# A gated short-convolution layer on one core: the first tile's shift and scale taken alone, the order of SyncE and VectorE in the first twelve passes written out, and half-size first pieces

## The chip, the cores and the metric

One Trainium2 core runs the whole layer in float32 inputs and outputs. The metric is the device time of one execution in microseconds (us), lower is better; of several runs the median is given. The engines are named as in the profile: PE (TensorE), DVE (VectorE), ACT (ScalarE), POOL (GpSimd), SP (SyncE, which issues almost all DMAs).

## The reference, cut to what matters

The depth is one, so only the short-convolution mixer runs, on 256 tokens of width 2048, with 4096 inner columns:

```
h = rmsnorm(x, norm_g)
shift, scale, gate = split(silu(c) @ ada_w + ada_b, 3)
h = h * (1 + scale) + shift
b, cg, v, g = split(h @ w_in, 4)          # w_in: 2048 x 16384
y = b * causal_conv3(cg * v) * silu(g)
x = x + gate * (y @ w_out)                # w_out: 4096 x 2048
out = rmsnorm(x, final_g)
```

The weights w_in (128 MB), ada_w (48 MB) and w_out (32 MB) are each read once.

## The kernel before, in words

**Products.** Every float32 product is made of three: a tile of weights is split into a rounded part `hi` (ACT, `split_hi`, L356) and a rest `lo` (DVE, `split_lo`, L361), the tokens likewise into `hh` and `hl` (both in the tile that the profile calls hT), and PE adds hi by hh, hi by hl and lo by hh in PSUM (`product`, L496). One such product has 128 x 128 weights and 256 tokens. The width of 2048 makes 16 token tiles, k = 0 to 15.

**Shift and scale of a token tile** are two rows of `silu(c) @ ada_w`, summed over the 16 row blocks of ada_w. For tiles 0 and 1 this is the front of the kernel: their 18 transfers are loaded first (L233), DVE multiplies and adds the row blocks up in `gv0` (L413, L415), PE sums four of the blocks (1, 11, 13 and half of 15) and at last `gv0` itself over the partitions into `sums0` (`sum0`, L394), DVE adds the bias into `mod` (`add_biases`, L326). Then ACT makes hh of both tiles from the normalised tokens `xs` (`high_tokens`, L330); DVE finishes tile 0 (`low_tokens`: xs at L334, hl at L337), and ACT (L429) and POOL (L433) finish tile 1. All of this is held in the order of the program by `in_order` (its last instruction on each engine is kept in `ended`).

The tiles from 2 on come in seven groups of two. `ada_piece` loads a piece of two row blocks by two transfers of 256 KB (L464), DVE adds them up (two operations a piece, L476 and L478), and after eight pieces `ada_done` has PE sum the group over the partitions (four transposes `tp_g`, L486), DVE reduce it (L487) and add the bias (L326), and `modulate` makes hh (ACT, L330) and hl (DVE, L334, L337).

**Passes.** While tiles become ready, PE works on one half of the columns (4 chunks by 4 quarters, 16 sums) in passes. A pass (`part`) loads weights for the tiles that are ready (`raw_s`, L540), splits them, makes the products in a PSUM bank `mm_s` and keeps the sum in SBUF (`keep`: ACT copies at L518, or DVE adds at L520; a pass may instead be seeded from the kept sum at L530). The first thirteen passes take tiles 0 and 1 alone: 24 products from 512 KB of weights each. The next three take four tiles, 48 products from one transfer of 1 MB each. After these 16 the same sums are taken up again for later tiles. Passes are counted here from 1; pass 1 uses weights loaded in the front (`raw0`, L198). Two passes of 512 KB share one buffer of 1 MB (`places`), of which there are three; of the `at` buffers of the ada pieces there are four.

**What sets the order.** `plan()` writes out once the order of pieces and passes. The scheduler, which orders each engine's instructions by priority and by its own timing, may leave that order: the DVE sums of a piece carry a lower priority (`later(GIVE)`), `ada_done` a higher one, and `behind` holds the splits of a pass behind one named instruction: hi behind the kept sum of three passes before, lo of the fourth and fifth pass behind a piece's sums (`added`). Between SP's loads of weights and of ada pieces there is no rule but that. After the passes PE makes the other half of the columns (`mm_b`, 3072 products), then the product with w_out (L738).

Of the kernel before, what the change touches and what calls it, by code (L numbers as in the profile page):

```python
# [8 lines left out]
F32 = mybir.dt.float32  # L9
# [4 lines left out]
P = 128  # L14
# [103 lines left out]
def short_conv_layer(ctx: ExitStack, tc: tile.TileContext, x, c, norm_g, ada_w, ada_b, w_in, conv_w, w_out, final_g, out):  # L118
# [44 lines left out]
    after = mybir.DependencyInfo(mybir.DependencyClass.NoSync, mybir.DependencyReason.DATA)  # L163

    @contextmanager
    def in_order():

        traced = nc.cur_bb.bb.instructions
        n = len(traced)
        yield  # L170
        last = {}
        for ins in list(traced[n:]):
            if ins.engine in last:
                tc.add_manual_dep(ins, last[ins.engine], after, reason="in order")
            last[ins.engine] = ins.name
        ended.update(last)

    @contextmanager
    def behind(last):
# [209 lines left out]
    def sum0(k, rows, col, halves=(0, 1)):  # L389


        for o in range(2 * NK0):
            if o // NK0 in halves:
                nc.tensor.matmul(  # L394
                    sums0[:, o * P : (o + 1) * P], rows[:, o // NK0, (o % NK0) * P : (o % NK0 + 1) * P],
                    col.to_broadcast([P, P]),
                    start=k == ON_PE[0] and o == 0, stop=k is None, skip_group_check=True,
                )

    for k in range(KT):  # L400
        c_k = silu_c[:, k : k + 1]
        at, gv = first_ada[k], gv0
        if k in ON_PE:
            if k == 11:
                for j in range(3):
                    keep_x(j, turn_x(j))
                tp_3 = turn_x(3)
            sum0(k, at, c_k, (0,) if k == KT - 1 else (0, 1))
            if k < KT - 1:
                continue  # L410
            at, gv = at[:, 1], gv0[:, 1]
        if k == 0:
            nc.vector.tensor_scalar_mul(gv, at, c_k)  # L413
        else:
            nc.vector.scalar_tensor_tensor(out=gv, in0=at, scalar=c_k, in1=gv, op0=ALU.mult, op1=ALU.add)  # L415
    for half in range(2):
        sum0(None, gv0, ones[:, 0:1], (half,))
    blocks0 = [raw0[:, k * CT * P : (k + 1) * CT * P] for k in range(NK0)]
    hi0 = [split_hi(b, CT * P) for b in blocks0]
    add_biases(0, NK0, sums0.rearrange("p (o f) -> p o f", o=2 * NK0)[:, :, 0])  # L420
    pieces0 = []
    for k in range(NK0):
        high_tokens(k)
    for k in range(NK0):
        if k == 0:
            pieces0.append(split_lo(blocks0[k], CT * P, hi0[k]))
            low_tokens(k)
        else:
            nc.scalar.activation(  # L429
                xs[0][:, k, :], xs[0][:, k, :], AF.Identity, bias=mod[:, 0, k : k + 1], scale=mod[:, 1, k : k + 1]  # L430
            )
            pieces0.append(split_lo(blocks0[k], CT * P, hi0[k]))
            nc.gpsimd.tensor_tensor(out=hl_[k], in0=xs[0][:, k, :], in1=hh_[k].bitcast(F32), op=ALU.subtract)  # L433
    pinned.close()

    def conv(ct, u, cv):
# [34 lines left out]
    def ada_sums(j, kk, at4, gv):  # L471
        for i in range(kk):
            c_k = silu_c[:, j + i : j + i + 1]
            if j + i == 0:
                with behind(ended):
                    nc.vector.tensor_scalar_mul(gv, at4[:, i], c_k)  # L476
            else:
                nc.vector.scalar_tensor_tensor(out=gv, in0=at4[:, i], scalar=c_k, in1=gv, op0=ALU.mult, op1=ALU.add)  # L478
        added.append({ins.engine: ins.name for ins in nc.cur_bb.bb.instructions[-1:]})

    def ada_done(k0, nk, gv):

        tp = psum.tile([P, 4, P], F32, tag="sm", name="tp_g", bufs=2)
        gs = const.tile([P, 4], F32, tag="gs", name="gs", bufs=2)
        for o in range(2 * nk):
            nc.tensor.transpose(tp[:, o, :], gv[:, o // nk, (o % nk) * P : (o % nk + 1) * P], ident)  # L486
        nc.vector.reduce_sum(gs[:, 0 : 2 * nk], tp[:, 0 : 2 * nk, :], axis=mybir.AxisListType.X)  # L487
        modulate(k0, nk, gs[:, 0 : 2 * nk])

    opener = [None]  # L490

# [20 lines left out]
    kept, added = [], []  # L512

    def keep(ch, q, k0, bank, seed=False):
        if k0 == 0 or seed:
# [6 lines left out]
    def part(ch, q, k0, k1, seed):  # L522


        col = q * E + ch * CT * P
        step = SLOT // (CT * P)
        first = k0
        bank = psum.tile([P, CT, T], F32, tag="mm", name="mm_s")
        if seed:
            nc.scalar.copy(bank, acc[ch, q])  # L530
        if pieces0:
            for k in range(NK0):
                chunk_products(bank, *pieces0[k], 0, k, k0, k1, late=True)
            pieces0.clear()
            k0 = NK0
        for s0 in range(k0, k1, step):
            sk = min(step, k1 - s0)
            n = sk * CT * P
            raw, hi, lo = places(n)
            nc.sync.dma_start(  # L540
                raw[:, :n].rearrange("p (k f) -> p k f", k=sk),
                w_in[0, s0 * P : (s0 + sk) * P, col : col + CT * P].rearrange("(k p) f -> p k f", p=P),
            )
            at = len(acc) if k0 == 0 else KT
            with behind(ended if at < 3 else kept[at - 3] if at < 9 else {}):
                split_hi(raw, n, hi)
            with behind(ended if at < 3 else added[at - 3] if at < 5 else {}):
                split_lo(raw, n, hi, lo=lo)
            for parts in ((0, 1), (2,)) if 0 < len(acc) < 3 else ((0, 1, 2),):
                for i in range(sk):  # L550
                    chunk_products(bank, hi, lo, i * CT * P, s0 + i, k0, k1, seed, parts=parts)
        if len(acc) == 1:
            with behind(ended):
                keep_x(3, tp_3)
        keep(ch, q, first, bank, seed)
        kept.append({ins.engine: ins.name for ins in nc.cur_bb.bb.instructions[-1:]})
# [14 lines left out]
            split_y(ys[-1], vq)  # L571

    LATER = (10, 14)
    whole = [0] * NCH
    for kind, *step in plan():
        if kind == "ada":
            ada_piece(*step)
        else:
            ch, k1 = step[0], step[3]
            part(*step)  # L580
            if step[2] == 0 and len(acc) in LATER:
                with tc.issue_after(last_mm[0].ins), behind(ended):
                    if len(acc) == LATER[0]:
                        rows2 = rows_tile("rows2")
                        nc.gpsimd.dma_start(rows2[:, :], conv_w.rearrange("w (k p) -> (w k) p", p=P))
                    else:
                        turn(rows2, 0, 96, cw)
            whole[ch] += k1 == KT
            if k1 == KT and whole[ch] == 4:
                mixed(ch)  # L590
# [354 lines left out]
```

## Time and profile before

| | |
|---|---|
| three runs | 902.77, 903.24 (median), 905.11 us |
| profiled execution | 903.37 us |
| its span, first to last instruction | 901.6 us |
| mean granted TensorE clock | 0.997 |
| PE busy | 887.4 us, 98% |
| first product of a pass | 25.01 us after the span's start |
| passes on the first half of the columns | to 378.57 us |
| the second half, mm_b | 348.16 us, 3072 products |

The profile is of one execution. A row of a timeline gives start, duration, engine, source line, operation, output and inputs, and in brackets the idle time before it and what ended that. Times are from the span's start; outside the span the profiled execution has another 1.8 us. PE is busy nearly all the time, so what can be gained or lost is time at which PE waits.

### The profile page before, as it was taken

The numbers are of one execution on the slowest core, as the hardware profiler recorded it, in microseconds if no ns is written. First come the engines' busy times: TensorE is split into PE (matmuls) and PEld (weight loads), VectorE is DVE, ScalarE is ACT, GpSimd is POOL, SyncE is SP. The second block draws the span as 40 slices with busy tenths as digits, with TensorE's granted clock in tenths as the row PEclk, the third lists the DMA queues.
The fourth block names the chain that finished last, engine by engine and source line by source line (L and its number), as shares of the span: only waits on it lengthen the run. The fifth ranks groups of instructions, "written<-read, shape, count | busy, mean of one in ns | idle before, by whom it ended". The sixth has DMA issues, their size and how long they took to land.

```text
span 901.6 us, 16416 instructions
## 1 busy us (share of the span) xinstructions
PE 887.4 (98%) x6997; PEld 850.6 (94%) x6997; DVE 675.3 (75%) x665; ACT 484.9 (54%) x429; POOL 84.8 (9%) x96
## 2 busy tenths in 40 slices
PE   7999999999999999999999999999999999999996
PEld 4899999999999999999999999999999988888885
DVE  5889989888888867765775678565555568879886
ACT  6768866665548856644443434444434445554543
POOL 0000000000000042024224302420000000000000
PEclk9999999999999999999999999999999999999998
DMA  9999999999998588687978898866666476673662
GB/s 307 365 369 368 368 315 348 356 369 352 351 326 289 165 277 250 192 257 229 295 227 247 256 289 269 240 198 197 201 193 188 141 284 222 199 275 123 203 234 94
DMA packets 159610, 235.01 MB, mean 261 GB/s; under 512 B 6900, under 2 KB 105284, under 8 KB 159152
## 3 DMA queue, kind: packets, MB, share of 16 engines
q1 hardware_dynamic: 156368, 226.52, 76.7%
q0 software_dynamic: 3040, 7.39, 2.8%
q8 instruction: 55, 0.90, 0.4%
q14 instruction: 19, 0.16, 0.1%
q10 hardware_dynamic: 128, 0.04, 0.0%
HBM read 224.49 MB, written 2.10 MB: 251 GB/s over the span
## 4 chain that ended last, share of the span: by engine, by line
PE 95%; DMA 3%; SPq 0%; ACT 0%; DVE 0%; issue 0%; ACTq 0%; DVEq 0%
PE mm_b L496 39%; PE mm_s L496 37%; PE mm_w L738 7%; PE mm_o L738 7%; PE mm L738 4%; DMA at<-in_ada_w_dram 2%; DMA x<-in_x_dram 1%; PE tp_g L486 0%; DVE lo L361 0%; SPq L464 0%; ACT hi L356 0%; ACT acc L518 0%; SPq L540 0%; SPq L218 0%; ACT big L852 0%
## 5 line engine op out<-in xcount | busy, mean ns | idle before, releaser
L496 PE MATMUL mm_s<-hT,hi 128*128 128x256 f32 x2048 | 348.4, 277 | 1.1 <-ACT hT L330 1.1
L496 PE MATMUL mm_b<-hT,hi 128*128 128x256 f32 x2048 | 348.2, 276 | 0.0
L496 PEld LDWEIGHTS mm_s<-hT,hi 128*128 128x128 f32 x2048 | 307.2, 188 | 1.3 <-ACT hT L330 1.3
L496 PEld LDWEIGHTS mm_b<-hT,hi 128*128 128x128 f32 x2048 | 308.2, 188 | 0.0
L496 PE MATMUL mm_b<-hT,lo 128*128 128x256 f32 x1024 | 282.8, 276 | 0.0
L496 PE MATMUL mm_s<-hT,lo 128*128 128x256 f32 x1024 | 280.2, 277 | 0.8 <-DVE lo L361 0.8
L356 ACT CAST hi<-raw 128x2048 fp32r<-128x2048 f32 (+1 forms) x66 | 123.7, 1875 | 193.5 <-PE mm_b L496 156.7
L361 DVE TENSOR_TENSOR lo<-raw,hi 128x2048 fp32r<-128x2048 f32 (+1 forms) x66 | 150.4, 2280 | 99.9 <-ACT hi L356 99.3
L496 PEld LDWEIGHTS mm_b<-hT,lo 128*128 128x128 f32 x1024 | 192.2, 188 | 0.0
L496 PEld LDWEIGHTS mm_s<-hT,lo 128*128 128x128 f32 x1024 | 190.7, 188 | 1.2 <-DVE lo L361 1.2
L361 DVE TENSOR_TENSOR lo<-raw_s,hi 128x2048 fp32r<-128x2048 f32 (+1 forms) x80 | 149.5, 1877 | 35.1 <-ACT hi L356 34.6
L356 ACT CAST hi<-raw_s 128x2048 fp32r<-128x2048 f32 (+1 forms) x80 | 124.2, 1558 | 58.2 <-PE mm_s L496 47.2
L478 DVE SCALAR_TENSOR_TENSOR gv<-at,silu_c,gv 128x512 f32<-128x512 f32 x105 | 78.5, 748 | 7.6 <-DMA at<-in_ada_w_dram 5.9
L518 ACT COPY acc<-mm_s 128x1024 f32<-128x1024 f32 x54 | 54.7, 1013 | 39.4 <-PE mm_s L496 39.2
L361 DVE TENSOR_TENSOR lo<-raw_o,hi 128x2048 fp32r<-128x2048 f32 x22 | 50.4, 2290 | 23.4 <-ACT hi L356 23.4
L356 ACT CAST hi<-raw_o 128x2048 fp32r<-128x2048 f32 x22 | 42.0, 1908 | 46.4 <-PE mm_w L738 12.6
L738 PE MATMUL mm_w<-hi,y 128*128 128x512 f32 x184 | 58.8, 389 | 0.0
L634 POOL TENSOR_TENSOR gacc<-gacc,z 128x512 f32<-128x512 f32 x28 | 44.7, 1597 | 116.2 <-DMA z<-gacc 116.2
L738 PE MATMUL mm_o<-hi,y 128*128 128x512 f32 x176 | 55.3, 389 | 0.0
L628 DVE SCALAR_TENSOR_TENSOR gacc<-at_g,silu_c,gacc 128x512 f32<-128x512 f32 x60 | 45.8, 764 | 8.2 <-DMA at_g<-in_ada_w_dram 7.2
L632 POOL DMA_DIRECT2D z<-gacc x28 | 15.6, 556 | 330.5 <-DVE acc L569 283.9
L738 PEld LDWEIGHTS mm_w<-hi,y 128*128 128x128 f32 x184 | 34.5, 188 | 7.2
(154 smaller groups left out, 689.4 us busy)
## 6 DMA issues: line engine op xcount, KB each, us to landing
raw<-in_sc_w_in_dram SPq DMA_DIRECT2D x64, 1024.0 KB, 5.8
raw_s<-in_sc_w_in_dram SPq DMA_DIRECT2D x47, 1024.0 KB, 8.3
raw_o<-in_sc_w_out_dram SPq DMA_DIRECT2D x32, 1024.0 KB, 5.3
at<-in_ada_w_dram SPq DMA_DIRECT2D x126, 256.0 KB, 7.9
raw_s<-in_sc_w_in_dram SPq DMA_DIRECT2D x33, 512.0 KB, 7.2
at_g<-in_ada_w_dram SPq DMA_DIRECT2D x32, 512.0 KB, 8.1
x<-in_x_dram SPq DMA_DIRECT2D x4, 512.0 KB, 6.3
big<-in_x_dram SPq DMA_DIRECT2D x2, 1024.0 KB, 8.2
```

Of the source, the lines that this page charges most:

```text
L356: nc.scalar.copy(hi[:, :n], raw[:, :n])
L361: last_low[0] = nc.vector.tensor_tensor(out=lo[:, :n], in0=raw[:, :n], in1=hi[:, :n].bitcast(F32), op=ALU.subtract)
L478: nc.vector.scalar_tensor_tensor(out=gv, in0=at4[:, i], scalar=c_k, in1=gv, op0=ALU.mult, op1=ALU.add)
L496: mm = last_mm[0] = nc.tensor.matmul(dst, w, h[k], start=begins and left, stop=ends, skip_group_check=True)
L518: nc.scalar.copy(acc[ch, q], bank)
L628: nc.vector.scalar_tensor_tensor(out=ga, in0=at3[:, i, :], scalar=s, in1=ga, op0=ALU.mult, op1=ALU.add)
L632: nc.gpsimd.dma_start(turned[0 : P - away], ga[away:P])
L634: nc.gpsimd.tensor_tensor(out=ga, in0=ga, in1=turned, op=ALU.add)
L738: nc.tensor.matmul(dst, y[a], b, start=opens and i == 0, stop=ends and i == 2, skip_group_check=True)
```

## The change

It has three parts.

1. **Front.** Tile 0 is taken alone. PE adds the last row block for tile 0 in shift and scale, and DVE for tile 1; `first_bias(0)` sums tile 0's part of gv0 over the partitions and adds its bias, then DVE itself makes hh of tile 0 from the tokens. ACT makes xs of tile 0 afterwards. Tile 1 follows: POOL makes its tokens (a tensor_scalar in place of the subtraction at L433), ACT rounds them into hh, and the lo parts and hl of both tiles are DVE's.
2. **Order.** From the second step of the plan to the twelfth pass SP and DVE follow the program's order, so the two sums of an ada piece stand on DVE, and its loads on SP, where the plan has them. The holds of the fourth and fifth pass behind `added` go; the lo parts of pass 15 are held behind the first later group's last token operation (`turned_to`).
3. **Pieces.** In the first 16 passes a piece is at most 512 KB, so passes 14 to 16 load and split twice 512 KB in place of once 1 MB.

```diff
-    def in_order():
+    def in_order(engines=None):
...
+            if engines is not None and ins.engine not in engines:
+                continue
...
-        ended.update(last)
+        if engines is None:
+            ended.update(last)
...
-            sum0(k, at, c_k, (0,) if k == KT - 1 else (0, 1))
+            sum0(k, at, c_k, (0,) if k == KT - 1 else range(NK0))
...
-            at, gv = at[:, 1], gv0[:, 1]
+            at, gv = at[:, :, P : NK0 * P], gv0[:, :, P : NK0 * P]
...
+    def first_tokens(k, engine, out):
+        engine.tensor_scalar(
+            out=out, in0=xs[0][:, k, :], scalar1=mod[:, 1, k : k + 1], scalar2=mod[:, 0, k : k + 1],
+            op0=ALU.mult, op1=ALU.add,
+        )
+    def first_rest(k):
+        pieces0.append(split_lo(blocks0[k], CT * P, hi0[k]))
+        nc.vector.tensor_tensor(out=hl_[k], in0=xs[0][:, k, :], in1=hh_[k].bitcast(F32), op=ALU.subtract)
...
+    first_bias(0)
+    hi0.append(split_hi(blocks0[0], CT * P))
+    first_tokens(0, nc.vector, hh_[0])
+    nc.scalar.activation(xs[0][:, 0, :], xs[0][:, 0, :], AF.Identity, bias=mod[:, 0, 0:1], scale=mod[:, 1, 0:1])
+    for k in range(1, NK0):
+        first_bias(k)
+        first_tokens(k, nc.gpsimd, xs[0][:, k, :])
+        hi0.append(split_hi(blocks0[k], CT * P))
+        nc.scalar.copy(hh_[k], xs[0][:, k, :])
+    for k in range(NK0):
+        first_rest(k)
...
-        step = SLOT // (CT * P)
+        step = (SLOT if k0 else HALF) // (CT * P)
...
-            with behind(ended if at < 3 else added[at - 3] if at < 5 else {}):
+            with behind(ended if at < 3 else turned_to[0] if at == 14 else {}):
...
+    PLANNED = 19
+    for n, (kind, *step) in enumerate(plan()):
+        if n == 1:
+            planned.enter_context(in_order((mybir.EngineType.SP, nc.vector.engine)))
+        elif n == PLANNED:
+            planned.close()
```

Line numbers after the change are higher: L359 and L364 are the splits, L495 the sums of a piece, L503 the reduction, L513 the products.

**Place 1, the front on DVE**, from the last sums of gv0 on, before (mod is shift and scale, hT of a token tile is hh or hl):

```order
L415 SCALAR_TENSOR_TENSOR gv_181<-at_127,silu_c,gv_181 128x256
L326 TENSOR_TENSOR mod<-sum_180,vec 128x2x2
L361 TENSOR_TENSOR lo<-raw_130,hi 128x512
L334 TENSOR_SCALAR xs_175<-xs_175,mod 128x256
L337 TENSOR_TENSOR hT<-xs_175,hT 128x256
L361 TENSOR_TENSOR lo<-raw_130,hi 128x512
```

The same place after the change:

```order
L418 SCALAR_TENSOR_TENSOR gv_181<-at_127,silu_c,gv_181 128x2x128
L427 TENSOR_TENSOR mod<-sum_180,vec 128x2
L430 TENSOR_SCALAR hT<-xs_175,mod 128x256
L427 TENSOR_TENSOR mod<-sum_180,vec 128x2
L364 TENSOR_TENSOR lo<-raw_130,hi 128x512
L437 TENSOR_TENSOR hT<-xs_175,hT 128x256
L364 TENSOR_TENSOR lo<-raw_130,hi 128x512
L437 TENSOR_TENSOR hT<-xs_175,hT 128x256
```

The bias is added for one tile at a time, hh of tile 0 stands before everything else of tile 1, and both hl are here.

**Place 2, passes 4 to 6.** On SP before the change (at_413, at_481 and at_516 are ada pieces; the first row is pass 4's weights, then pass 5's, then those of passes 6 and 7):

```order
L540 DMA raw_s_381<-in_sc_w_in_dram 128x2x512
L464 DMA at_413<-in_ada_w_dram 128x2x256 x2
L540 DMA raw_s_381<-in_sc_w_in_dram 128x2x512
L464 DMA at_481<-in_ada_w_dram 128x2x256 x2
L464 DMA at_516<-in_ada_w_dram 128x2x256 x2
L540 DMA raw_s_449<-in_sc_w_in_dram 128x2x512 x2
```

And after it:

```order
L557 DMA raw_s_382<-in_sc_w_in_dram 128x2x512
L481 DMA at_414<-in_ada_w_dram 128x2x256 x2
L557 DMA raw_s_382<-in_sc_w_in_dram 128x2x512
L557 DMA raw_s_450<-in_sc_w_in_dram 128x2x512
L481 DMA at_482<-in_ada_w_dram 128x2x256 x2
L557 DMA raw_s_450<-in_sc_w_in_dram 128x2x512
L481 DMA at_517<-in_ada_w_dram 128x2x256 x2
```

Pass 6's weights now stand directly behind pass 5's, ahead of four ada transfers of 256 KB. On DVE, before (lo_383 is pass 4's and then pass 5's, lo_451 that of passes 6 and 7):

```order
L476 TENSOR_SCALAR gv_374<-at_375,silu_c_144 128x512
L478 SCALAR_TENSOR_TENSOR gv_374<-at_375,silu_c_144,gv_374 128x512
L478 SCALAR_TENSOR_TENSOR gv_374<-at_413,silu_c_144,gv_374 128x512
L361 TENSOR_TENSOR lo_383<-raw_s_381,hi_382 128x1024
L478 SCALAR_TENSOR_TENSOR gv_374<-at_413,silu_c_144,gv_374 128x512
L361 TENSOR_TENSOR lo_383<-raw_s_381,hi_382 128x1024
```

And after:

```order
L493 TENSOR_SCALAR gv_375<-at_376,silu_c_144 128x512
L495 SCALAR_TENSOR_TENSOR gv_375<-at_376,silu_c_144,gv_375 128x512
L364 TENSOR_TENSOR lo_384<-raw_s_382,hi_383 128x1024
L495 SCALAR_TENSOR_TENSOR gv_375<-at_414,silu_c_144,gv_375 128x512 x2
L364 TENSOR_TENSOR lo_384<-raw_s_382,hi_383 128x1024
L364 TENSOR_TENSOR lo_452<-raw_s_450,hi_451 128x1024
```

Pass 4's lo no longer stands behind the first sum of the piece that is loaded after it.

**Place 3, where the first two later groups are finished.** On PE the four transposes of the first group (tiles 2 and 3) stood behind 265 products and stand now behind 302; the first product that needs tile 2's hl is the 338th before and the 340th now. Those of the second group (tiles 4 and 5) stood behind 516 and stand now behind 552; the next lo that PE needs behind them is wanted by the 579th product in both. ACT at the first group, before (acc31 is pass 13's sum, hi_754 and hi_819 the weights of passes 14 and 15):

```order
L356 CAST hi_754<-raw_s_753 128x2048
L330 ACTIVATE hT_173<-xs0_175,mod_179 128x256 x2
L518 COPY acc20_695<-mm_s_664 128x1024
L518 COPY acc31_744<-mm_s_716 128x1024
L356 CAST hi_819<-raw_s_818 128x2048
```

And after (hi_755 and hi_823 are those weights):

```order
L535 COPY acc20_696<-mm_s_665 128x1024
L359 CAST hi_755<-raw_s_754 128x1024
L535 COPY acc31_745<-mm_s_717 128x1024
L359 CAST hi_823<-raw_s_822 128x1024
L333 ACTIVATE hT_173<-xs0_175,mod_179 128x256 x2
```

The hh of tiles 2 and 3 moved behind the copy of pass 13's sum and behind a hi. DVE at the second group, before (lo_1143 is the lo of the 579th product):

```order
L361 TENSOR_TENSOR lo_1110<-raw_s_1108,hi_1109 128x1024
L487 TENSOR_REDUCE gs_1057<-tp_g_1056 128x4
L326 TENSOR_TENSOR mod_179<-gs_1057,vec_142 128x2x2
L478 SCALAR_TENSOR_TENSOR gv_1100<-at_1196,silu_c_144,gv_1100 128x512 x2
L361 TENSOR_TENSOR lo_1143<-raw_s_1141,hi_1142 128x2048
```

And after (there it is lo_1153, and lo_1220 is wanted by the 604th product):

```order
L503 TENSOR_REDUCE gs_1067<-tp_g_1066 128x4
L495 SCALAR_TENSOR_TENSOR gv_1110<-at_1206,silu_c_144,gv_1110 128x512
L364 TENSOR_TENSOR lo_1153<-raw_s_1151,hi_1152 128x2048
L329 TENSOR_TENSOR mod_179<-gs_1067,vec_142 128x2x2
L495 SCALAR_TENSOR_TENSOR gv_1110<-at_1211,silu_c_144,gv_1110 128x512
L364 TENSOR_TENSOR lo_1220<-raw_s_1218,hi_1219 128x2048
```

The reduction, which waits for PE's transposes, is directly ahead of a sum and that lo, and the transposes come 36 products later than before.

More of the change, by code (lines that the diff above doesn't have):

```diff
@@ L415, in short_conv_layer, with first_bias @@
             nc.vector.scalar_tensor_tensor(out=gv, in0=at, scalar=c_k, in1=gv, op0=ALU.mult, op1=ALU.add)
[L416 to L417 removed]
     blocks0 = [raw0[:, k * CT * P : (k + 1) * CT * P] for k in range(NK0)]
[L419 to L433 removed]
+    hi0 = []
+    def first_bias(k):
+        sum0(None, gv0, ones[:, 0:1], (k,))
+        both = sums0.rearrange("p (s k f) -> p s k f", s=2, k=NK0)[:, :, k, 0]
+        nc.vector.tensor_tensor(out=mod[:, :, k], in0=both, in1=bias[:, :, k], op=ALU.add)
+    def first_tokens(k, engine, out):
[6 more added lines that the diff above has]
+        nc.vector.tensor_tensor(out=hl_[k], in0=xs[0][:, k, :], in1=hh_[k].bitcast(F32), op=ALU.subtract)
+    pieces0 = []
+    first_bias(0)
[7 more added lines that the diff above has]
+        nc.scalar.copy(hh_[k], xs[0][:, k, :])
+    for k in range(NK0):
+        first_rest(k)
     pinned.close()
@@ L488, in ada_done @@
         modulate(k0, nk, gs[:, 0 : 2 * nk])
+        turned_to.append({ins.engine: ins.name for ins in nc.cur_bb.bb.instructions[-1:]})
     opener = [None]
@@ L573, in short_conv_layer @@
     LATER = (10, 14)
+    PLANNED = 19
     whole = [0] * NCH
-    for kind, *step in plan():
+    planned = ExitStack()
+    for n, (kind, *step) in enumerate(plan()):
[3 more added lines that the diff above has]
+            planned.close()
         if kind == "ada":
```

7 lines of the change are left out of this document (3 added, 4 removed).

## The prediction

> **What bounds the kernel now.** I read the page first, then PE's waits, then the chain of work in order of time, then the timelines of all engines from 20 to 90 us.
>
> ```profile
> span 901.6 us, 16416 instructions
> PE 887.4 (98%) x6997; PEld 850.6 (94%) x6997; DVE 675.3 (75%) x665; ACT 484.9 (54%) x429; POOL 84.8 (9%) x96
> ...
> PE mm_s L496 <- ACT hT L330: 1.1, 1, 1.1
> PE mm_s L496 <- DVE lo L361: 0.8, 2, 0.5
> ...
> 378.57 348.16 PE mm_b L496 x3072
> ```
>
> PE is the bound: the longest part of the chain is 348.16 us for 3072 products without a gap, 0.1133 us each. Beside the start, PE waits inside the products only twice, 0.8 us in all. So a change of the order can give back little: the front's wait and those two. It can take more, by new waits.
>
> **The front.** Rows of PE, DVE, ACT and POOL:
>
> ```profile
> 22.70 1.23 PE L394 MATMUL sum<-ones,gv 128*128 128x128 f32 x8
> 25.01 0.74 PE L496 MATMUL mm_s<-hT,hi 128*128 128x256 f32 x4 [1.08 <-ACT hT L330]
> 27.43 2.43 PE L496 MATMUL mm_s<-hT,hi 128*128 128x256 f32 x20
> ...
> 21.11 2.06 DVE L415 SCALAR_TENSOR_TENSOR gv<-at,silu_c,gv 128x512 f32<-128x512 f32 x3 [0.45 <-DMA at<-in_ada_w_dram]
> 23.97 0.16 DVE L326 TENSOR_TENSOR mod<-sum,vec 128x4 f32<-128x4 f32 x1 [0.80 <-PE sum L394]
> 24.05 0.69 DVE L361 TENSOR_TENSOR lo<-raw,hi 128x512 fp32r<-128x512 f32 x1
> 24.99 0.41 DVE L334 TENSOR_SCALAR xs<-xs,mod 128x256 f32<-128x256 f32 x1 [0.25 <-ACT hT L330]
> 25.44 0.42 DVE L337 TENSOR_TENSOR hT<-xs,hT 128x256 fp32r<-128x256 f32 x1
> ...
> 23.10 1.36 ACT L356 CAST hi<-raw 128x512 fp32r<-128x512 f32 x2 [1.72 <-DVE gv L415]
> 24.36 1.09 ACT L330 ACTIVATE hT<-xs,mod 128x256 fp32r<-128x256 f32 x2
> 25.48 0.60 ACT L429 ACTIVATE xs<-xs,mod 128x256 f32<-128x256 f32 x1
> ...
> 26.17 0.90 POOL L433 TENSOR_TENSOR hT<-xs,hT 128x256 fp32r<-128x256 f32 x1 [24.86 <-ACT xs L429]
> ```
>
> Before, the sums over the partitions come in two fours; the second waits for DVE's last gv operation (21.11 + 2.06 = 23.17) and ends at 23.93, so four take 0.76. Now tile 0's four need only the operation ahead of that, as the first four did at 22.70: they end at 23.46. The add (0.16) follows at about 23.5; a DVE operation that needs the one before starts 0.04 after its end (24.99 + 0.41, then 25.44), so hh of tile 0 runs from 23.70 to 24.11, and PE starts 0.05 later (ACT's first hT ends at 24.36 + 0.60 = 24.96, PE's row is 25.01). ACT's hi is there by 23.8. **First product 24.16 instead of 25.01.**
>
> Behind it DVE has tile 1's add (0.08 to the next row's start) and lo (0.69), so PE's lo products can start at 24.93, while four products from 24.16 end at 24.7: 0.2 us of wait. A wait costs 0.11 more, since the second product after it comes 0.23 and not 0.11 later (33.98 and 34.21 below). Tile 0 then ends at 25.94. Tile 1's hh needs POOL's tensor_scalar, which the trace does not show. The nearest row is POOL's subtraction of the same shape, 0.90; I take that: 24.27 + 0.90, then ACT's rounding 0.60, ready at 25.85, just in time. Bounds: 0 and twice the row, 1.80. At 0 nothing changes; at 1.80 hh is 0.8 late. Pass 1 ends at 25.94 + 12 x 0.113 = 27.30; before it ended at 27.43 + 4 x 0.113 = 27.88 (the first 4 of those 20 are its last). **Lead 0.6.**
>
> The Trainium skill, "GPSIMD Engine Reference", Engine selection, says that a one-input operation on GpSimd runs at roughly line rate and a two-input one about half as fast as on VectorE. By it POOL's operation would take about half of 0.90, an estimate of 0.45, and the sum would stay the same, since hh is in time at 0.90 already. No run here shows it.
>
> **The two waits, passes 4 and 6.**
>
> ```profile
> 33.98 0.39 PE L496 MATMUL mm_s<-hT,lo 128*128 128x256 f32 x1 [0.27 <-DVE lo L361]
> 34.21 0.39 PE L496 MATMUL mm_s<-hT,hi 128*128 128x256 f32 x2
> 40.24 0.39 PE L496 MATMUL mm_s<-hT,lo 128*128 128x256 f32 x1 [0.53 <-DVE lo L361]
> ...
> 32.04 0.75 DVE L478 SCALAR_TENSOR_TENSOR gv<-at,silu_c,gv 128x512 f32<-128x512 f32 x1 [1.44 <-DMA at<-in_ada_w_dram]
> 32.71 1.22 DVE L361 TENSOR_TENSOR lo<-raw_s,hi 128x1024 fp32r<-128x1024 f32 x1
> ...
> 30.49 1.05 ACT L356 CAST hi<-raw_s 128x1024 fp32r<-128x1024 f32 x1
> 33.48 1.05 ACT L356 CAST hi<-raw_s 128x1024 fp32r<-128x1024 f32 x1 [1.03 <-DMA raw_s<-in_sc_w_in_dram]
> 36.80 1.02 ACT L518 COPY acc<-mm_s 128x1024 f32<-128x1024 f32 x1 [1.37 <-PE mm_s L496]
> 37.88 1.05 ACT L356 CAST hi<-raw_s 128x1024 fp32r<-128x1024 f32 x1
> ...
> 30.00:35.00 5.00, 4.73 (x41) 4.54 (x41) 3.56 (x5) 3.97 (x6) 0.00 (x0) 1.00 1.08 354
> 35.00:40.00 5.00, 4.71 (x42) 4.52 (x40) 4.73 (x6) 3.33 (x4) 0.00 (x0) 1.00 1.05 383
> 85.00:90.00 5.00, 5.00 (x46) 5.00 (x46) 4.93 (x7) 4.17 (x5) 0.00 (x0) 1.00 1.07 364
> ```
>
> The last three rows are five-microsecond stretches; their last number is the DMA's GB/s, and the queues never run dry here (busy share over 1).
>
> Pass 4: its weights land as before (ACT's row at 30.49), and its lo (32.71) stood behind a sum that waited 1.44 for its DMA. That sum now stands behind it: hi to 31.54, lo 31.6 to 32.8. PE arrives at 27.30 + 48 x 0.1133 = 32.74, needs lo with the third product at 32.97, and does not wait. Before, it went on at 33.98 + 0.11: lead 1.1. Pass 5: its weights land at 33.48 in both, hi to 34.53, lo to 35.8, PE at 35.86; it arrives at 32.97 + 24 x 0.1133 = 35.69, waits 0.17 and pays 0.11. It goes on from 35.97; before from 34.09 + 2.72 = 36.81: lead 0.8. Pass 6: before, hi began at 37.88, behind four ada transfers and a copy, and PE went on at 40.24 + 0.11. Now its 512 KB come straight behind pass 5's, 0.524 MB at 375 GB/s or 1.4 us later: landed at 34.9, hi to 35.95, lo (DVE is free at 35.8) to 37.2, and PE wants it at 35.97 + 2.72 = 38.69. **Lead 40.35 - 38.69 = 1.66 us.** Pass 5 eats most of the front's part: were the front not faster at all, pass 6 would be reached at 38.99, and the lead would be 1.36.
>
> From here to pass 13 a step takes 512 KB of weights and mostly 512 KB of ada, 2.8 us at 375 GB/s, against 2.72 of products; the 1.4 us in hand shrink by about 0.1 a pass and suffice. SP in the plan's order may block on a buffer, but an issue lands a median 8.2 us later (last row below), so the stream does not stop for it.
>
> Pieces of 512 KB in passes 14 to 16: same bytes, and ACT and DVE pay twice a start (2 x 1.05 for 1.92, 2 x 1.22 for 2.29), 0.2 each, three times. I cost it at nothing: ACT waits for PE there anyway. Without that cover it is 0.6.
>
> The Trainium skill, "DMA: Bandwidth & Descriptors", section Bandwidth, speaks against this: it asks for 1 MiB or more per DMA. By its table (1 MB in 6.15 us, 64 KB in 0.95) six halves might cost some 0.4 us each, an estimate. The rows differ: 383 GB/s in the stretch from 35 us, where pieces were 512 KB, 364 in that from 85 us, where they were 1 MB.
>
> **The new waits, at place 3.**
>
> ```profile
> 85.90 0.44 PE tp_g L486 x4
> ...
> 57.75 0.68 DVE L487 TENSOR_REDUCE gs<-tp_g 128x4 f32<-128x512 f32 x1
> 60.08 2.29 DVE L361 TENSOR_TENSOR lo<-raw_s,hi 128x2048 fp32r<-128x2048 f32 x1
> 62.28 0.74 DVE L478 SCALAR_TENSOR_TENSOR gv<-at,silu_c,gv 128x512 f32<-128x512 f32 x1
> ...
> ACT acc L518 <- PE mm_s L496: 14.6, 13, 2.6
> ...
> raw_s<-in_sc_w_in_dram SPq DMA_DIRECT2D x12, 512.0 KB, 8.2
> ```
>
> Both chains start from PE, so a lead does not help. Queued operations on ACT and DVE overlap by 0.1 (two of 0.60 take 1.09).
>
> First group: pass 13 ends with product 312. ACT copies its sum from 0.2 after product 313 starts (0.3 from a product's start, as at 36.80), then a hi, then hh of tile 2, then DVE xs and hl: 0.2 + 0.92 + 0.95 + 0.60 + 0.04 + 0.45 + 0.42 + 0.05 = 3.63. PE wants hl with product 340, 27 x 0.1133 = 3.06 later. Wait 0.57 + 0.11 = **0.68**. Before, hh stood ahead of the copy and 72 products lay behind the transposes.
>
> Second group: from the start of the transposes, 0.65 to the reduction (0.34 to the last of four, 0.31 of latency), then reduction 0.59, sum 0.65, lo 2.29 and 0.05: 4.23. PE takes 0.53 for the transposes (0.44, and 0.09 to come back) and 26 products, 2.95: 3.48. Wait 0.75 + 0.11 = **0.86**. The lo behind it comes 0.07 + 0.65 + 2.2 = 2.9 later, 25 products take 2.83 + 0.11: no wait. Before, 62 products, 7 us, lay between. From the third group on the transposes stand where they stood.
>
> **Sum**, against the profiled execution: 903.37 - 1.66 + 0.68 + 0.86 = 903.25. That execution is 0.13 above the runs' median of 903.24, so I predict **903.1**: the lead is earned and given back.
>
> **Rivals.**
> - *The lead is kept.* If place 3 costs nothing, 903.24 - 1.66 = 901.6. For it: every DVE or ACT row is within 0.1 of what it must beat by 0.6 or 0.8 only if several sums leave the chain. Against: the order is fixed, and all durations are quoted. Half of it gives 902.3. Chance 0.17.
> - *Slower, by the DMA's rate.* VectorE's lo now always waits behind both sums of the piece loaded ahead of it, so a late ada transfer holds PE. It decides when six steps with a piece eat the 1.4 us in hand, 0.24 a pass: 1.05 MB in 2.95 us, 355 GB/s. The stretch from 30 to 35 us had 354, the next 383. At 340 (3.08 us) PE waits about 0.8 and 0.3 of restarts: 904.2. With a third wait like the second group's, 905. Chance 0.2.
> - *Slower, by POOL*, at 1.80: pass 1 ends 0.8 later, pass 5 takes 0.2 of it back: 903.7. Chance 0.04.
> - *Halves cost DMA time*, as by the skill's rule: if six halves ran at 354 and not 364 GB/s, 3.1 MB come 0.25 us later, with the 0.6 of ACT and DVE 0.85 at most: 904.0. The rows are against it. Chance 0.03.
> - *The change does not do what it says*: the front still starts at 25.0 because something else is last, 903.4. Chance 0.04.
>
> **Numbers.** The forecast has 0.52 (902.4 to 903.9). About 0.3%, 2.7 us, can be told from no change. All there is to win is 0.85 and the two waits with their restarts, 0.81 + 0.22, or more by the transfers' order up to 2.2: not 2.7, so faster has 0.02. Slower by 2.7 needs four waits like those of place 3: 0.06. Range 901.3 to 904.8: below, the kept lead, and pass 5's wait (0.17 + 0.11) gone besides; above, the DMA case.
>
> **What would show it.** First product at about 24.2; no wait at pass 4 or 6, one of 0.2 at pass 5; at about 40 us PE 1.6 ahead; waits of 0.5 to 0.9 for hT at 64 us and for lo at 92; from 100 us on the same products at the same times as before, within 0.3; mm_b again 348.2. A wait for DMA in passes 7 to 13 would make the second rival right; no waits at 64 and 92 the first.

## The result, and the profile after

**Slower by 0.16%:** median 904.70 us over 22 runs (904.20 to 905.15), before 903.23 us over 22 runs; ratio 1.0016, 95% interval 1.0010 to 1.0022. The profiled execution took 904.69 us, 1.32 more than that of before (903.37).

The page of the changed kernel, its first lines:

```profile
span 902.9 us, 16425 instructions
PE 888.4 (98%) x6997; PEld 851.1 (94%) x6997; DVE 672.4 (74%) x670; ACT 483.1 (54%) x431; POOL 92.8 (10%) x96
```

PE is busy 1.0 us longer for the same 6997 instructions. Where the time went is told by the start of the same product in both traces (products of the passes counted from 1, us from the span's start):

| | before | after | after - before | step |
|---|---|---|---|---|
| product 1 | 25.01 | 23.95 | -1.06 | -1.06 |
| product 14 (the second of tile 1) | 26.64 | 26.77 | +0.13 | +1.19 |
| product 124 (pass 6, behind its first lo) | 40.47 | 39.23 | -1.24 | -1.37 |
| product 613 | 97.10 | 97.55 | +0.45 | +1.69 |
| first product of mm_b | 378.40 | 379.23 | +0.83 | +0.38 |
| last product of mm_b | 726.45 | 727.51 | +1.06 | +0.23 |
| last product of all | 894.01 | 895.01 | +1.00 | -0.06 |
| end of the span | 901.59 | 902.91 | +1.32 | +0.32 |

**The front.** Rows of DVE, PE, ACT and POOL after the change:

```profile
23.39 0.41 DVE L430 TENSOR_SCALAR hT<-xs,mod 128x256 fp32r<-128x256 f32 x1
24.09 0.16 DVE L427 TENSOR_TENSOR mod<-sum,vec 128x2 f32<-128x2 f32 x1 [0.28 <-PE sum L397]
24.17 0.69 DVE L364 TENSOR_TENSOR lo<-raw,hi 128x512 fp32r<-128x512 f32 x1
...
23.34 0.71 PE L397 MATMUL sum<-ones,gv 128*128 128x128 f32 x4 [0.25 <-DVE mod L427]
23.95 0.71 PE L513 MATMUL mm_s<-hT,hi 128*128 128x256 f32 x4
24.91 0.72 PE L513 MATMUL mm_s<-hT,lo 128*128 128x256 f32 x4 [0.25 <-DVE lo L364]
26.55 0.72 PE L513 MATMUL mm_s<-hT,hi 128*128 128x256 f32 x4 [0.46 <-ACT hT L448]
...
23.84 0.60 ACT L443 ACTIVATE xs<-xs,mod 128x256 f32<-128x256 f32 x1 [0.39 <-DVE hT L430]
26.09 0.40 ACT L448 CAST hT<-xs 128x256 fp32r<-128x256 f32 x1 [1.14 <-POOL xs L430]
...
24.44 1.61 POOL L430 TENSOR_SCALAR xs<-xs,mod 128x256 f32<-128x256 f32 x1 [23.13 <-ACT xs L443]
```

The first product comes 1.06 earlier in these two profiles. Profiles of like kernels differ by some tenths here: over all profiles, those of the experiments with them, it starts at 24.70 to 25.01 with the front of before (six profiles) and at 23.95 to 24.20 with the new one (five), so some 0.8 is the work of the change. Then PE stops twice. The lo products start at 24.91, 0.42 late and 0.11 for the restart: DVE's add for tile 1, ahead of that lo, waits 0.28 for PE's sums. Tile 1 starts at 26.55, another 0.62 and 0.11: POOL's tensor_scalar starts only when ACT's xs of tile 0 ends (23.84 + 0.60) and takes 1.61, and ACT can round hh only behind it. At product 14 the lead is gone.

**Passes 4 to 6.** The same two stretches as before the change (the columns are PE, PEld, DVE, ACT and POOL, then PEclk, DMA share and GB/s):

```profile
30.00:35.00 5.00, 5.00 (x46) 5.00 (x46) 4.21 (x6) 4.58 (x8) 0.00 (x0) 1.00 1.06 366
35.00:40.00 5.00, 5.00 (x46) 5.00 (x46) 4.52 (x6) 3.82 (x5) 0.00 (x0) 1.00 1.08 365
```

PE is busy throughout, where 0.27 and 0.29 of these stretches were idle before (the second wait, 0.53 by its row, ran on past 40 us). Both waits are gone, and the lead is there again, 1.24 us.

**Place 3.** PE's rows at the two waits, then what ACT did ahead of the first and DVE ahead of the second:

```profile
64.76 0.39 PE L513 MATMUL mm_s<-hT,hi 128*128 128x256 f32 x1 [0.40 <-DVE hT L340]
93.44 0.39 PE L513 MATMUL mm_s<-hT,lo 128*128 128x256 f32 x1 [0.64 <-DVE lo L364]
...
61.33 1.02 ACT L535 COPY acc<-mm_s 128x1024 f32<-128x1024 f32 x1 [1.24 <-PE mm_s L513]
62.25 1.05 ACT L359 CAST hi<-raw_s 128x1024 fp32r<-128x1024 f32 x1
63.20 1.09 ACT L333 ACTIVATE hT<-xs,mod 128x256 fp32r<-128x256 f32 x2
...
89.83 0.69 DVE L503 TENSOR_REDUCE gs<-tp_g 128x4 f32<-128x512 f32 x1 [1.52 <-PE tp_g L502]
90.44 0.74 DVE L495 SCALAR_TENSOR_TENSOR gv<-at,silu_c,gv 128x512 f32<-128x512 f32 x1
91.10 2.28 DVE L364 TENSOR_TENSOR lo<-raw_s,hi 128x2048 fp32r<-128x2048 f32 x1
```

By the starts of the products the first wait is 0.57 and the second 0.80, each with 0.11 for the restart. These two, 1.59 together, give back more than the lead. A little more, 0.08, is lost at product 605, straight behind the first use of the next lo.

**Behind 100 us.** Here nothing was to happen. PE lost 0.31 at 286.6 us and 0.2 at 548.1, with no releaser named:

```profile
286.40 0.72 PE L513 MATMUL mm_s<-hT,hi 128*128 128x256 f32 x4
287.05 0.39 PE L513 MATMUL mm_s<-hT,lo 128*128 128x256 f32 x1
...
547.87 0.39 PE L513 MATMUL mm_b<-hT,hi 128*128 128x256 f32 x2
548.18 0.39 PE L513 MATMUL mm_b<-hT,lo 128*128 128x256 f32 x1
```

The four products from 286.40 would have been followed at 286.85, the two from 547.87 at 548.10; a restart follows each. The last is the end: from the last product to the end of the span 7.90 us, and 7.59 before. SP's last instructions (L941 before, L964 after; the drains come when all its DMAs have landed) stand 1.3 us later behind a last product 1.0 us later:

```profile
L941 SPq DRAIN  x3: 7/7/7, 900.8 to 901.1; - x3
...
L964 SPq DRAIN  x3: 7/7/7, 902.1 to 902.4; - x3
```

### The profile page after: what moved, and what is told of

Same layout as the page of the kernel before. It is cut to its first block, busy times and chain, and to the rows that moved or that the text cites. A ratio compares the mean times of both kernels' runs of the same rounds, so it can differ in the third digit from the quotient of the medians.

```text
span 902.9 us, 16425 instructions
## 1 busy us (share of the span) xinstructions
PE 888.4 (98%) x6997; PEld 851.1 (94%) x6997; DVE 672.4 (74%) x670; ACT 483.1 (54%) x431; POOL 92.8 (10%) x96
## 4 chain that ended last, share of the span: by engine, by line
PE 96%; DMA 2%; DVE 0%; ACT 0%; issue 0%; SPq 0%; POOL 0%; ACTq 0%; DVEq 0%
PE mm_b L513 39%; PE mm_s L513 38%; PE mm_w L761 7%; PE mm_o L761 7%; PE mm L761 4%; DMA at<-in_ada_w_dram 2%; PE tp_g L502 0%; DVE lo L364 0%; SPq L221 0%; POOL xs L430 0%; PE sum L397 0%; ACT hi L359 0%; ACT big L875 0%; ACTq L964 0%; ACT xs L443 0%
## 5 line engine op out<-in xcount | busy, mean ns | idle before, releaser
L513 PE MATMUL mm_s<-hT,hi 128*128 128x256 f32 x2048 | 348.8, 277 | 0.9 <-ACT hT L448 0.5
L513 PE MATMUL mm_b<-hT,hi 128*128 128x256 f32 x2048 | 348.3, 276 | 0.0
L513 PEld LDWEIGHTS mm_s<-hT,hi 128*128 128x128 f32 x2048 | 307.5, 188 | 1.3 <-ACT hT L448 0.7
L513 PEld LDWEIGHTS mm_b<-hT,hi 128*128 128x128 f32 x2048 | 308.4, 188 | 0.0
L513 PE MATMUL mm_b<-hT,lo 128*128 128x256 f32 x1024 | 282.8, 276 | 0.0
L513 PE MATMUL mm_s<-hT,lo 128*128 128x256 f32 x1024 | 280.1, 277 | 0.9 <-DVE lo L364 0.9
L359 ACT CAST hi<-raw 128x2048 fp32r<-128x2048 f32 (+1 forms) x66 | 123.7, 1875 | 193.5 <-PE mm_b L513 146.6
L364 DVE TENSOR_TENSOR lo<-raw,hi 128x2048 fp32r<-128x2048 f32 (+1 forms) x66 | 150.8, 2287 | 100.9 <-ACT hi L359 100.6
L513 PEld LDWEIGHTS mm_b<-hT,lo 128*128 128x128 f32 x1024 | 192.2, 188 | 0.1
L513 PEld LDWEIGHTS mm_s<-hT,lo 128*128 128x128 f32 x1024 | 190.6, 188 | 1.4 <-DVE lo L364 1.3
L364 DVE TENSOR_TENSOR lo<-raw_s,hi 128x1024 fp32r<-128x1024 f32 (+1 forms) x83 | 149.7, 1808 | 43.4 <-ACT hi L359 43.0
L359 ACT CAST hi<-raw_s 128x1024 fp32r<-128x1024 f32 (+1 forms) x83 | 124.6, 1509 | 57.1 <-PE mm_s L513 48.9
L495 DVE SCALAR_TENSOR_TENSOR gv<-at,silu_c,gv 128x512 f32<-128x512 f32 x105 | 78.5, 748 | 1.7
L364 DVE TENSOR_TENSOR lo<-raw_o,hi 128x2048 fp32r<-128x2048 f32 x22 | 50.4, 2291 | 22.7 <-ACT hi L359 22.5
L359 ACT CAST hi<-raw_o 128x2048 fp32r<-128x2048 f32 x22 | 42.0, 1908 | 45.8 <-PE mm_w L761 14.8
L657 POOL TENSOR_TENSOR gacc<-gacc,z 128x512 f32<-128x512 f32 x28 | 50.2, 1794 | 119.2 <-DMA z<-gacc 119.2
```

The costliest lines, as they stand in the source:

```text
L359: nc.scalar.copy(hi[:, :n], raw[:, :n])
L364: last_low[0] = nc.vector.tensor_tensor(out=lo[:, :n], in0=raw[:, :n], in1=hi[:, :n].bitcast(F32), op=ALU.subtract)
L513: mm = last_mm[0] = nc.tensor.matmul(dst, w, h[k], start=begins and left, stop=ends, skip_group_check=True)
L657: nc.gpsimd.tensor_tensor(out=ga, in0=ga, in1=turned, op=ALU.add)
```

## The experiments

My theory after the result: each part does what its own chains of DVE and ACT say; the order wins 1.3 us, the front loses what it wins, and place 3 takes the rest. The rivals: POOL's operation alone is the loss; the half pieces cost transfer time; the order of SP and DVE costs by itself. All ratios are to the kernel before.

### Tile 1's hh by ACT, all else as changed

```diff
-        first_tokens(k, nc.gpsimd, xs[0][:, k, :])
+        high_tokens(k)
         hi0.append(split_hi(blocks0[k], CT * P))
-        nc.scalar.copy(hh_[k], xs[0][:, k, :])
+        nc.scalar.activation(
+            xs[0][:, k, :], xs[0][:, k, :], AF.Identity, bias=mod[:, 0, k : k + 1], scale=mod[:, 1, k : k + 1]
+        )
```

> The change with tile 1's hh made by ACT again (ACT makes hh and then xs; POOL does nothing in the front); all else as changed. Theory, that the lead is lost in three waits of PE (tile 1's hh at 25.8 us, hT at 64, lo at 92): the wait at 25.8 goes, so product 13 comes 0.73 us earlier; pass 5 then waits up to 0.4 for its lo, since its weights land when they did; the waits at 64 and 92 stay as they are (0.57 and 0.80). 903.9 to 904.5. Rival, that POOL's 1.61 us is the whole loss: 903.2 or less. Rival, that the front has nothing to do with it: 904.7.

904.31 us, ratio 1.0011 (1.0002 to 1.0019). PE's rows:

```profile
24.33 0.71 PE L515 MATMUL mm_s<-hT,hi 128*128 128x256 f32 x4
25.29 0.72 PE L515 MATMUL mm_s<-hT,lo 128*128 128x256 f32 x4 [0.25 <-DVE lo L364]
25.85 1.07 PE L515 MATMUL mm_s<-hT,hi 128*128 128x256 f32 x8
```

The wait for tile 1 is gone: its four hi products join those of tile 0 in one row of eight. Product 25 starts at 27.66 and not 28.02, but product 124 at 39.10 and not 39.23: pass 4's lo takes 0.2 of it back. The waits at 64 and 92 are again 0.56 and 0.80. So POOL's operation is part of the loss and not the whole: 0.39 of the 1.47 in the median. The intervals of the two ratios overlap, so the rows say this more surely than the times.

### Pieces of 1 MB, all else as changed

```diff
-        step = (SLOT if k0 else HALF) // (CT * P)
+        step = SLOT // (CT * P)
```

> The change with pieces of 1 MB again in passes 14 to 16; all else as changed. Theory (chains of DVE and ACT set the time): splitting 1 MB before the first product of pass 14 takes 1.92 + 2.29 us and not 1.05 + 1.22, so PE waits 2 to 2.5 us for lo at about 61 us; hT at 64 and perhaps lo at 92 are then in time (0.68 and 0.91 back). 905.3 to 905.9. Rival, that transfers of 512 KB are what costs: 904.0 or less.

905.07 us, ratio 1.0025 (1.0017 to 1.0034), a little under what the theory gave and far from the rival. Rows of PE, ACT and DVE, then stretches of PE alone (busy time and count, PEclk, DMA share, GB/s):

```profile
61.41 0.39 PE L513 MATMUL mm_s<-hT,hi 128*128 128x256 f32 x2
64.11 0.41 PE L513 MATMUL mm_s<-hT,lo 128*128 128x256 f32 x1 [2.30 <-DVE lo L364]
...
59.30 1.90 ACT L359 CAST hi<-raw_s 128x2048 fp32r<-128x2048 f32 x1
61.76 2.29 DVE L364 TENSOR_TENSOR lo<-raw_s,hi 128x2048 fp32r<-128x2048 f32 x1
...
61.00:64.00 3.00, 0.80 (x7) 1.00 1.06 379
64.00:65.00 1.00, 0.90 (x5) 0.67 1.08 363
65.00:66.00 1.00, 1.00 (x6) 0.50 1.09 351
66.00:67.00 1.00, 1.00 (x7) 0.50 1.10 353
67.00:68.00 1.00, 1.00 (x8) 0.63 1.05 364
68.00:69.00 1.00, 1.00 (x11) 1.00 1.06 386
```

One wait of 2.47 us for lo stands where the changed kernel had two, and neither of those appears. So the half pieces are needed with the new order: without them this wait costs more than both. The profiled execution, 906.54, shows something more: behind the wait PE ran at half its clock for some 3.4 us, and 1.7 us more were lost. The eleven times lie in two heaps, seven from 904.75 to 905.16 and four from 906.54 to 906.75. The mean granted clock is 0.996 in three of these four and 0.997 or 0.998 in the seven, so I take it that the clock fell in three of the eleven; the fourth (906.75) has 0.999, and why it took longer is not shown. The Trainium skill, "TensorE: Matmul & The Clock Gate", Part 1, has the clock halved after an idle window of about 3.4 us; here a wait of 2.3 us by PE's rows was enough for it. None of the waits of the changed kernel, 0.8 at most, shows it.

### The change with the front of before

The kernel before, with parts 2 and 3 of the change (the lines are against the changed kernel):

```diff
-    first_bias(0)
-    hi0.append(split_hi(blocks0[0], CT * P))
-    first_tokens(0, nc.vector, hh_[0])
...
+    hi0 = [split_hi(b, CT * P) for b in blocks0]
+    add_biases(0, NK0, sums0.rearrange("p (o f) -> p o f", o=2 * NK0)[:, :, 0])
```

> The change's order and half pieces with the front of before. Theory: first product at 25.0 as before, no wait at passes 4 and 6 (1.35 us of lead at product 123), waits of 0.4 to 0.6 for hT at 64 us and 0.2 to 0.8 for lo at 92; as POOL's 1.61 us is not there, no worse than the whole change: 902.5 to 903.7. Rival, that SP's and DVE's order costs by itself (DMA or engine queues): 904.5 or more.

903.32 us, ratio 1.0002 (0.9993 to 1.0011). First product at 24.97, product 124 at 39.06 with no wait between: the order alone wins 1.4 us to there (40.47 before), 0.2 more than with the new front. The wait at 64 is the same 0.57; that at 92 is 0.19 and not 0.80, since the second group's transposes stand behind 539 products and not 552. So **the new front costs some 1.4 us in the median** (904.70 with it), and most of that is far from the front. In the two profiles 0.17 of it stands at product 124 and 0.61 at the wait at 92 us, as the scheduler's order came out another way 60 us later; another 0.5 is lost at 286.6 and 548.1 us, where this profile has no loss.

### The front alone

The changed kernel without `planned` and with the holds and the 1 MB pieces of before:

```diff
-        if n == 1:
-            planned.enter_context(in_order((mybir.EngineType.SP, nc.vector.engine)))
...
-            with behind(ended if at < 3 else turned_to[0] if at == 14 else {}):
+            with behind(ended if at < 3 else added[at - 3] if at < 5 else {}):
```

> The change's front with the order, holds and 1 MB pieces of before. Theory: the first product at about 24.0, tile 1's hh late at 25.8, then the same waits at passes 4 and 6, whose end is set by transfers and not by PE, take up whatever the front gained or lost: 903.2, within 0.3. Rival, that the front is what makes the change slower: 904.3 to 904.7. Rival, that the front's 0.85 is kept: 902.4.

903.34 us, ratio 1.0005 (0.9996 to 1.0014). PE's row where pass 6 waits, and ACT's ahead of it:

```profile
40.09 0.39 PE L513 MATMUL mm_s<-hT,lo 128*128 128x256 f32 x1 [0.37 <-DVE lo L364]
...
36.81 1.02 ACT L535 COPY acc<-mm_s 128x1024 f32<-128x1024 f32 x1 [1.71 <-PE mm_s L513]
37.72 1.06 ACT L359 CAST hi<-raw_s 128x1024 fp32r<-128x1024 f32 x1
```

First product at 24.10, tile 1 late at 26.70, product 25 at 28.22 (27.89 before). Pass 4 then does not wait, and the wait of pass 6 ends at 40.09, where it ended at 40.24 before: what the front lost is swallowed by these waits. I had expected that a transfer sets the end of the second one. In the profile of before it does: pass 6's weights land at 37.80, and hi starts at 37.88. Here they land at 37.20, and hi starts behind ACT's copy of pass 4's sum, which waits for PE. So it is not shown that a gain or loss of any size would be swallowed here. Only with the new order, where nothing waits at passes 4 and 6, does the front's loss reach the end.

### Both waits of place 3 taken away

Two holds are added to the changed kernel:

```diff
+            if k == NK0:
+                first_hh.update({ins.engine: ins.name for ins in nc.cur_bb.bb.instructions[-1:]})
...
+        if k0 == 2 * NK0:
+            turned_pe.append({ins.engine: ins.name for ins in nc.cur_bb.bb.instructions[-1:]})
...
+                    with behind(turned_pe.pop() if turned_pe else {}):
+                        chunk_products(bank, hi, lo, i * CT * P, s0 + i, k0, k1, seed, parts=parts)
...
+        with behind(first_hh if len(acc) == 12 else {}):
+            keep(ch, q, first, bank, seed)
```

> The change, with two holds more: ACT's copy of pass 13's sum waits until tile 2's hh is made, and the first product of the pass behind the second later group waits until that group's transposes are done (they then stand behind 528 and not 552 products). Theory: the waits for hT at 64 us (0.57 + 0.11 in the changed kernel's profile) and for lo at 92 (0.80 + 0.11) both go and nothing takes their place: 904.7 - 1.6 = 903.1, 902.8 to 903.5. Rival, that new waits take their place or that the lead goes elsewhere: 904.2 to 904.9.

902.88 us, ratio 0.9998 (0.9989 to 1.0007): 1.8 us less than the changed kernel. ACT at 60 us, and DVE ahead of the lo that was late at 92:

```profile
62.84 1.10 ACT L333 ACTIVATE hT<-xs,mod 128x256 fp32r<-128x256 f32 x2 [1.71 <-DVE mod L329]
63.85 0.99 ACT L540 COPY acc<-mm_s 128x1024 f32<-128x1024 f32 x1
...
87.08 0.68 DVE L508 TENSOR_REDUCE gs<-tp_g 128x4 f32<-128x512 f32 x1
89.34 2.28 DVE L367 TENSOR_TENSOR lo<-raw_s,hi 128x2048 fp32r<-128x2048 f32 x1
```

hh now waits for `mod` alone and stands ahead of the copy; 0.13 and a restart are left at 64 us. The reduction comes 2.7 us earlier, lo 1.8, and nothing waits at 92. Both chains were named rightly. From product 124 to 613 this profile takes 56.78 us, and that of the changed kernel 58.32: 1.54 of the 1.8. The late weight loads of PE at 286 and 548 us are also gone in this profile.

### The end: eight more DMAs in place of three

Half pieces make three more DMAs of SP. Here two loads of the gate's bias become seven, in the changed kernel:

```diff
-        nc.sync.dma_start(
-            gates[j].rearrange("p a f -> p (a f)"),
-            ada_b[0:1, 2 * D + j * 1024 : 2 * D + (j + 1) * 1024].partition_broadcast(P),
-        )
+        cuts = ((0, 256, 512, 768, 1024), (0, 512, 768, 1024))[j]
+        for a, b in zip(cuts, cuts[1:]):
+            nc.sync.dma_start(
+                gates[j].rearrange("p a f -> p (a f)")[:, a:b],
+                ada_b[0:1, 2 * D + j * 1024 + a : 2 * D + j * 1024 + b].partition_broadcast(P),
+            )
```

> The change, with two loads of the gate's bias cut into seven, so that SP issues eight DMAs more than before and not three. Theory: at the end SP waits for its DMA semaphores one by one, 0.06 us each, in a fixed order, and which of the eight the last output has goes round with the count of DMAs; three more put it third and five waits behind it, eight more put it last again. Last product to the end of the span 7.6 us and not 7.9; the rest as changed: 904.4, 904.1 to 904.6. Rival, that the longer end is chance or comes with the half pieces themselves: 7.9, 904.7.

904.66 us, ratio 1.0018 (1.0009 to 1.0027). From the last product to the end it is 7.64 us, as expected. The median did not follow: it is that of the changed kernel, as the rival had it, and why is not shown (in this profile PE loses 0.2 more at 842 us, but that is one execution). In all 13 profiles the end goes by the count of DMAs:

| DMAs more than before | last product to end of span, us |
|---|---|
| 0 (before, pieces of 1 MB, front alone) | 7.59, 7.63, 7.59 |
| 3 (after, and five others) | 7.90, 7.90, 7.91, 7.89, 7.91, 7.91 |
| 8 (three kernels, one of them twice) | 7.64, 7.67, 7.61, 7.60 |

In the trace before, SP passes its last semaphore 6.69 us behind the last product and drains; after, it passes that of the last output at 6.70 and then five more, 0.06 each. The eight semaphores go round with the DMAs, and SP waits for them in a fixed order.

### Half pieces alone

```diff
-        step = SLOT // (CT * P)
+        step = (SLOT if k0 else HALF) // (CT * P)
```

> The kernel before with the half pieces alone. Theory: the waits at passes 4 and 6 as before, place 3 without a wait, the end 0.3 longer by the count of DMAs: 903.5, 903.2 to 903.9 (up to 0.5 of it late weight loads of PE with no wait behind them, as at 286.6 us in the changed kernel). Rival, that six halves cost transfer time: 904.0 or more, with PE waiting for lo or hi in passes 14 to 16.

903.28 us, ratio 1.0001 (0.9992 to 1.0010). No wait in passes 14 to 16; the end is 7.91. Up to there the order is that of before, and yet pass 4 waits only 0.05 (0.43 before, by the starts of the products), since the ada transfer for which DVE waits lands 0.4 earlier: how long PE waits at pass 4 differs from execution to execution. The rule of the Trainium skill, "DMA: Bandwidth & Descriptors", section Bandwidth, asks for 1 MiB or more per DMA; six halves in place of three show no cost here that can be measured.

### The front of before, both holds, eight more DMAs

The order and half pieces of the change with the front of before, the two holds of the run with both waits taken away, and the seven loads of the gate's bias.

> The front of before, the change's order and half pieces, the two holds of the run with both, and the seven loads of the gate's bias. Theory: no wait of PE from product 1 on to 100 us; 903.3 for order and pieces with the front of before, less 0.57 + 0.11, less 0.19 + 0.11, less 0.3 at the end: 902.0, 901.7 to 902.6. Rival, that the waits are replaced by others: 903.0 or more.

901.84 us, ratio 0.9983 (0.9974 to 0.9992). The stretch from 60 to 100 us, of the changed kernel and of this one (PE's busy time and count of matmul records):

```profile
60.00:100.00 40.00, 38.96 (x339) 1.00 1.06 359
```

```profile
60.00:100.00 40.00, 40.00 (x355) 1.00 1.07 369
```

The second has no wait, and no wait in the passes at all. This is faster than both kernels: 1.4 us less than before the change and 2.9 less than after it.

### Is an earlier front worth anything now?

Three kernels beside one another: the last one with the new front and tile 1's hh by ACT; the last one with the gate's bias in two loads again; and the last one again.

> The change's front with tile 1's hh by ACT, the change's order and half pieces, the two holds and the seven loads of the gate's bias: the run with the front of before (901.84), but the first product some 0.5 us earlier. Theory: a front that is earlier is taken back by pass 1's own lo and by passes 4 to 6, whose weights land when they did, so product 123 comes no earlier: 901.6 to 902.2. Rival, that the front's lead is kept once nothing behind it waits: 901.2 to 901.4.

> As the run with the front of before, both holds and eight more DMAs, but with the gate's bias in two loads as before, so three more DMAs. Theory: last product to end 7.9 us and not 7.7, all else alike: 0.25 more, 902.0 to 902.3. Rival, that the place in the round of semaphores does not show in the time of a run: 901.8.

> The same kernel as the run with the front of before, both holds and eight more DMAs, once more beside the two others: 901.84 again within 0.2 if what was measured is the kernel and not the chip.

902.01 us, ratio 0.9983 (0.9974 to 0.9991); 902.15 us, ratio 0.9984 (0.9975 to 0.9993); 901.85 us, ratio 0.9986 (0.9976 to 0.9995). PE's rows in the first of the three:

```profile
24.36 0.71 PE L520 MATMUL mm_s<-hT,hi 128*128 128x256 f32 x4
25.33 0.74 PE L520 MATMUL mm_s<-hT,lo 128*128 128x256 f32 x4 [0.26 <-DVE lo L367]
```

Its first product comes 0.54 earlier than in the second of the three (24.90), and the fifth waits 0.42 and 0.11, 0.53 in all, for lo. From there PE does not wait up to the pass at 64 us, so passes 4 to 6 take nothing, other than I had expected; pass 1's own lo takes it all. An earlier hh without an earlier lo is worth nothing. The three more DMAs cost 0.3 in the median here, as the end of the profile says (7.91 and 7.6); the ratios do not tell these two kernels apart.

The profiled execution of the third took 905.26, 3.4 us over its median, and shows where that went: PE waited four times between 524 and 549 us, the two longest times for a late lo. The longest:

```profile
537.47 0.39 PE L504 MATMUL mm_b<-hT,lo 128*128 128x256 f32 x1 [1.82 <-DVE lo L367]
```

The granted clock stayed at 1.00 behind this wait.

## Why the prediction was wrong

The forecast was 0.1 us faster; it became 1.47 us slower, inside the range but on the other side. Against the profiled execution the sum was -0.12 and came out at +1.32, 1.44 apart:

- **The lead, -1.66 forecast, -1.24 measured: 0.42 of the error.** The step that failed is this one: "The nearest row is POOL's subtraction of the same shape, 0.90; I take that". The operation took 1.61. It also began 0.49 behind the first product and not 0.11, since DVE's add for tile 1 waited for PE's sums and POOL then for ACT's xs. So hh, written as just in time, made PE wait 0.62 and 0.11. The bound of 1.80 and its rival (903.7, chance 0.04) had the right mechanism; I took the nearest row although it is another operation with two inputs. The first product was nearly right (0.85 earlier forecast, some 0.8 over all profiles). But lo came 0.42 late; I wrote 0.2, and my own rows gave 0.32, as four products from 24.16 end at 24.61. The lead that I wrote for a front that is not faster at all, 1.36, came out at 1.41 in the run with the front of before. The size of the lead is uncertain by some 0.4, as profiles of like kernels differ: product 124 stands at 39.23 in this profile and at 39.32 and 39.48 in two others with the same front, order and pieces, and at 40.47 before and 40.10 with half pieces alone.
- **Passes 4 to 6:** the waits at 4 and 6 went, as written; the 0.17 at pass 5 did not come, PE came there later.
- **Place 3, +1.54 forecast, +1.69 measured: 0.15.** Waits of 0.57 and 0.75 were forecast, 0.57 and 0.80 measured, and in four kernels the first was 0.56 to 0.57 whatever the lead. That "a lead does not help" where both chains start from PE is shown by this, and by the run without the two.
- **"From 100 us on the same products at the same times": 0.55.** The late weight loads at 286.6 and 548.1 us, 0.51 together, were in no step.
- **The end: 0.31.** "Same bytes", I wrote of the half pieces, and costed three more DMAs at nothing. They cost it at the end, in every profile.
- **The rivals.** The DMA's rate was wrong: 366 and 365 GB/s in the two stretches, and no wait for weights. The halves' cost in transfer time was wrong as well; the estimate of 0.4 us for each half does not come out of its two figures either (a straight line through them gives 0.3). The kept lead would have needed place 3 without a price; with that made so, the change is at 902.88.

The size of the error in the profile is told by these terms, and 0.86 of the 1.44 lies in two that were put at nothing. The sign in the medians hangs on the front: without it, order and pieces are even with before.

**Open:** what makes PE's weight loads late at 286.6 us (in the three profiled kernels that have the new front, the new order and both waits of place 3, each time at products 2260 to 2262, and in no other) and at 548.1 (in the changed kernel alone). In the trace a 16 KB transfer of instructions ends at 286.7, in the middle of the first, and another at 548.1; the kernels without the loss have such transfers too, one of them ending at 286.8 (in the run with both waits taken away). No run isolates it. Open too is why the median did not follow the shorter end in the changed kernel.

## What to carry to other kernels

Time won upstream reaches the end only where every later chain has slack, and a chain that starts from the bound engine itself has the same slack however early it starts: look for those before counting a lead. When one part of an edit is bound by a wait that another part removes, the first part's loss comes to light: try the parts apart. An operation that no trace shows goes where being late costs nothing, or is measured by itself first.

## What the runs showed of the hardware that I had not expected

- POOL's tensor_scalar of 128x256 took 1.61 to 1.62 us in five kernels, its subtraction of two inputs 0.90; DVE takes 0.41 and 0.42 for the same two. The Trainium skill, "GPSIMD Engine Reference", Engine selection, has one input at about line rate and two inputs about twice as slow as on VectorE; by it the estimate was 0.45. The trace agrees for two inputs and not for one.
- A wait of PE of 2.3 us was followed by half the clock for 3.4 us and cost 1.7 us more (by the granted clock in three of eleven executions, the profiled one among them). A wait of 1.8 us in another kernel was not.
- Which semaphore the last output DMA has decides 0.3 us at the end of the kernel.
